# Linear attention: decays, state updates and token loads queued by edges behind the next level's preparation, and a ramp that splits weights behind tokens

## The chip, the cores and the metric

The kernel runs on one core of a Trainium2 chip. The time is device microseconds of one execution: 2990.07 us as the median of three runs (2988.25 to 2991.81). TensorE is called PE here (its weight loads PEld), VectorE DVE, ScalarE ACT, GpSimd POOL, and the engine that issues the DMAs SP.

## The reference

One layer of a diffusion transformer over 2048 latent tokens and 256 context tokens of width 1024. Gated linear attention (4 heads, key width 64, value width 128, both directions), retention, and a mixture of 16 experts follow one another. The change touches the linear attention alone, whose chunk step is this:

```python
b = jnp.cumsum(gc, axis=2)
decay = jnp.exp(jnp.where(mask, b[:, :, :, None, :] - b[:, :, None, :, :], -jnp.inf))
scores = jnp.einsum('bhik,bhjk,bhijk->bhij', qc, kc, decay)
o = jnp.einsum('bhij,bhjv->bhiv', scores, vc) + jnp.einsum('bhik,bhkv->bhiv', qc * jnp.exp(b), s)
s = jnp.exp(b_end)[:, :, 0, :, None] * s + jnp.einsum('bhjk,bhjv->bhkv', kc * jnp.exp(b_end - b), vc)
```

The tokens enter as `h = rmsnorm(x) * (1 + scale) + shift`, where scale and shift are `silu(c) @ w_ada`.

## The kernel before

Every float32 product is made of three products of rounded halves (hi times hi, hi times lo, lo times hi), so each weight and each token tile is split by a cast on ACT (`split`, L136) and a subtraction on DVE (L137).

The linear attention goes through blocks of 256 tokens, two chunks of 128 tokens in each: block 0 is the context, blocks 1 to 8 the latent tokens. `H(b)` loads a block of tokens, squares and scales them (`load`), transposes them (`pt`), modulates (`ht`), splits them (`hhi`, `hlo`) and stores them to DRAM (`hThi`, `hTlo`). `PJ(b)` makes the projections (`pk`, `pq` into `kq`; `pz` into `zt`; `pv` into `v`). `PRO(ci)` has six pieces for a chunk: G is the gate (`pg`, `ab`, `la`), C the running sums (`pcs`, `cc`), E the decayed keys (`ke`), T their transposition (`pkt`, `kd`), I the state update (`pi`, `gstate`), Q the decayed queries (`qe`, stored as `g_qe`).

`LV(ci)` computes the scores of a chunk in seven levels of half sizes 64 to 1. `prep(l)` subtracts on POOL (`dd`, L540 and L541), takes the exponential on ACT (L542), multiplies by keys and queries on DVE (`bq`, L545), and copies parts into the zero-padded `az` on ACT (L546) and POOL (L547). `level(l)` is the product `pscr` on PE and its masked copy into `st` (on ACT for level 0, L573, on DVE after, L575). `fin` is the product `po` of scores and values, copied to `ot` and stored.

The `run` lists write down the order of PE: each step's PE instructions are tied by `tc.issue_after` behind the last PE instruction before. That edge binds PE alone. A scheduler places the instructions of ACT, DVE, POOL and SP by their order in the code and by when it expects each to be ready. `tc.issue_after(ins)` gives every instruction in its block that runs on the engine of `ins` an order edge behind `ins`. An engine executes its queue in order, so an instruction that waits holds what is behind it.

The ramp is what lies before block 1. The modulation weights `ada` pass through PE (`pmod`), are copied out (`mr`, L262), transposed (`pmt`) and turned into `gsc` and `bsc`, without which no token can be modulated. The first weights of the projections are `wk` (keys), `wv` (two halves), `wq`, each loaded as two tiles `raw` of 512 KB (two buffers) and split into `whi` and `wlo`; `wz` is the small gate weight, three casts and a subtraction from `wz_raw`.

Of the kernel before, what the change touches and what calls it, by code (L numbers as in the profile page):

```python
# [8 lines left out]
F32 = mybir.dt.float32  # L9
# [5 lines left out]
OP = mybir.AluOpType  # L15
# [3 lines left out]
P = 128  # L19
# [48 lines left out]
def kernel_body(ctx, tc, a, cst, out, dbg=None, stop=None):  # L68
# [155 lines left out]
    with ExitStack() as ph:  # L224
# [36 lines left out]
        for n in range(4):  # L261
            (S.copy if n % 2 else V.tensor_copy)(mr2[:, n], pm[n][0:4])  # L262
        pmt = ptr([P, 16, 2, 2], "pmt")
# [11 lines left out]
        V.tensor_scalar(nsgn, sgn, -1.0, None, op0=OP.mult)  # L275
        wk = load_w(w_in, 3616, C_GK, W1, rp=(ad, "ada"))
        wz_raw = ad.tile([P, KC, 32], F32, name="wz_raw", tag="ada")
        wz_i = SY.dma_start(wz_raw, rows_ap(w_in, C_GZ, [[3616, P], [P * 3616, KC], [1, 32]]))

        wz_r = wz_raw.rearrange("p k (d r) -> p k d r", d=2)  # L280
        for n in range(3):
            S.copy(wz[:, :, :, n], wz_r)
        Q.tensor_tensor(wz[:, :, :, 3], wz_r, wz[:, :, :, 0].bitcast(F32), op=OP.subtract)


    with gw:
# [11 lines left out]
        w2 = g1.tile([66, 2, 256], F32R)  # L298
        w2_raw = gl.tile([66, 2, 256], F32, name="w2_raw", tag="bq", bufs=3)
        held.enter_context(tc.issue_after(wz_i.ins))  # L300
        w2_lo = gl.tile([66, 2, 256], F32R, name="w2_lo", tag="bq", bufs=3)
# [3 lines left out]
        SY.dma_start(w2_raw[64:66], rows_ap(ggb, 0, [[0, 2], [256, 2], [1, 256]]))  # L305
        split(w2, w2_lo, w2_raw, copy=V.tensor_copy, eng=Q)
        SY.dma_start(w2[16:32].bitcast(F32), w2_lo[16:32].bitcast(F32))
# [19 lines left out]
        cur = [0]  # L327
        hs, blk, chk, last = {}, {}, {}, {}

        def H(b, xs=None):  # L330
# [17 lines left out]
            def part(k2):  # L348
                def f():
# [6 lines left out]
                    for k in range(2):  # L356
# [4 lines left out]
                        else:  # L361
                            V.tensor_scalar(ht[:, k], pt[:, k], g_, b_, op0=OP.mult, op1=OP.add)
                    split(r["hi"][:, 2 * k2:2 * k2 + 2], r["lo"][:, 2 * k2:2 * k2 + 2], ht)
                return f
# [156 lines left out]
        def LV(ci):  # L521
# [5 lines left out]
            def prep(l):  # L527
                def f():
# [9 lines left out]
                    if h > 1:  # L538
                        ref = c4[:, :, h - 1:h]
                        Q.tensor_tensor(d4[:, :, h:], c4[:, :, h:], ref.to_broadcast([P, 4 * nb, h]), op=OP.subtract)  # L540
                        Q.tensor_tensor(d4[:, :, :h], ref.to_broadcast([P, 4 * nb, h]), c4[:, :, :h], op=OP.subtract)  # L541
                        S.activation(dd, dd, AF.Exp)  # L542


                        V.tensor_tensor(halves_of(bq, h), halves_of(dd, h), halves_of(kq, h), op=OP.mult)  # L545
                        S.copy(v4(az[l], F_, lo_), v4(bq, F_, lo_))  # L546
                        Q.tensor_copy(v4(az[l], B_, up_), v4(bq, B_, up_))  # L547
                    else:

                        kf, qf, kb, qb = kq[F_, 0], kq[F_, 1], kq[B_, 1], kq[B_, 0]  # L550
                        Q.tensor_tensor(d4[:, :, 0:1], c4[:, :, 1:2], c4[:, :, 0:1], op=OP.subtract)
                        S.activation(d4[:, :, 1:2], d4[:, :, 0:1], AF.Exp)
                        w4 = lambda x_, s_: x_.rearrange("p a (n x) -> p (a n) x", n=nb)[:, :, s_]
                        S.copy(v4(az[l], F_, lo_), w4(kf, lo_))
                        Q.tensor_copy(v4(az[l], B_, up_), w4(kb, up_))
                        S.mul(v4(bq, F_, lo_), w4(qf, lo_), 2.0)
                        S.mul(v4(bq, B_, up_), w4(qb, up_), 2.0)
                        V.tensor_tensor(v4(bq, F_, up_), v4(dd, F_, up_), w4(qf, up_), op=OP.mult)
                        V.tensor_tensor(v4(bq, B_, lo_), v4(dd, B_, up_), w4(qb, lo_), op=OP.mult)
                    r[l] = bq  # L560
# [25 lines left out]
            return [prep(l) for l in range(7)], [level(l) for l in range(7)], fin  # L586

        def run(*steps):

# [19 lines left out]
        h0 = H(0, xs0)  # L609
        for f in h0[:-1]:  # L610
            f()
        wv = [load_w(w_in, 3616, C_GV + 256 * i, W1) for i in range(2)]
        h0[-1]()
# [41 lines left out]
        for b in range(1, nblk):  # L655
# [6 lines left out]
            else:  # L662
                kq, z, vn, nx = [none] * 8, [none] * 2, [none] * 8, {"G": none, "C": none, "E": none}
            (_, m, f_), (pn, _, _), p, p0, p1 = lv[2 * b], lv[2 * b + 1], lv[2 * b][0], pro[2 * b], pro[2 * b + 1]
            run(fin, v[2], p[2], m[0], p1["G"], h[1], v[3], p[3], p0["T"], m[1], p0["Q"], h[2], v[4], p[4], m[2], h[3],
                p1["C"], v[5], p[5], m[3], h[4], h[5], p0["I"], p[6], m[4], v[6], pn[0], m[5], v[7], pn[1], p1["E"],
                m[6])
            fin, p, m = f_, pn, lv[2 * b + 1][1]
            pn = lv[2 * b + 2][0] if more else [none] * 2
            run(p[2], m[0], z[0], fin, z[1], kq[0], p[3], m[1], hn[0], p1["T"], p1["Q"], kq[1], kq[2], p[4], m[2],  # L670
                nx["G"], kq[3], kq[4], p[5], m[3], p1["I"])
            if b == nblk - 2:
                early_w(C_RV)
            if b == nblk - 1:
                early_w(C_RQ)
            run(kq[5], p[6], m[4], nx["C"], kq[6], kq[7], pn[0], m[5], vn[0], pn[1], nx["E"], m[6], vn[1])
            if b == nblk - 2:
# [943 lines left out]
```

## Time and profile before

| what | value |
|---|---|
| median of three runs | 2990.07 us |
| the profiled execution | 2996.73 us |
| its span in the trace | 2994.9 us |
| mean granted clock of PE | 0.979 of full speed |
| PE busy | 2842.5 us, 95% |
| DVE busy | 1953.5 us, 65% |
| ACT busy | 1304.9 us, 44% |
| POOL busy | 514.6 us, 17% |
| mean DMA rate | 185 GB/s |

The ramp takes the first 98 us or so, the linear attention of blocks 1 to 8 lasts to 540 us, retention and the output projection follow up to about 1000 us, and the rest is the router and the experts. A block takes 54 to 56 us. Shares of the whole span say little on a change that acts in a sixth of it; the stretch from 100 to 545 us has to be read by itself.

### The profile page before, as it was taken

The page shows a single profiled execution, that of the slowest core. Times are in us where ns is not written, and L with a number is a line of the kernel's source. Part 1 is how long each engine was busy: PE and PEld are TensorE (multiplying, and loading weights), DVE is VectorE, ACT ScalarE, POOL GpSimd, SP SyncE. Part 2 cuts the span into 40 slices and gives each one's busy share as a digit, 9 for nine tenths or more (in the row PEclk, how much of TensorE's full clock was granted, in tenths as well). Part 3 has the DMA queues.
Part 4 walks back from the last instruction along what each step waited for, and adds up shares of the span by engine and source line. Part 5 has one row for each costly group of instructions (what it writes and reads, how often), then busy time and mean ns, then how long its engine had stood idle before and what let it go on. Part 6 is the DMA issues. An engine that isn't in the chain of part 4 may idle for free.

```text
span 2994.9 us, 55113 instructions
## 1 busy us (share of the span) xinstructions
PE 2842.5 (95%) x21597; PEld 2687.6 (90%) x21597; DVE 1953.5 (65%) x4264; ACT 1304.9 (44%) x2310; POOL 514.6 (17%) x636
## 2 busy tenths in 40 slices
PE   6898988899999999997999999999999999999997
PEld 4888888899889999996889999999999999999996
DVE  6777777667676666656877565556565565556557
ACT  7677676332222211112334444444444444444454
POOL 1355455233121110111110000000000000000000
PEclk8999999999999999998999999999999999999999
DMA  8212114689876544434665666666566666666676
GB/s 283 79 74 113 71 64 145 204 257 275 261 226 191 180 137 131 135 102 151 202 192 181 207 209 202 201 204 219 180 219 207 203 205 197 195 203 215 200 243 247
DMA packets 458024, 554.74 MB, mean 185 GB/s; under 512 B 21126, under 2 KB 392402, under 8 KB 455460
## 3 DMA queue, kind: packets, MB, share of 16 engines
q1 hardware_dynamic: 448260, 516.61, 53.4%
q0 software_dynamic: 9504, 34.61, 4.5%
q8 instruction: 170, 2.79, 0.4%
q14 instruction: 90, 0.74, 0.1%
HBM read 458.03 MB, written 93.08 MB: 184 GB/s over the span
## 4 chain that ended last, share of the span: by engine, by line
PE 76%; DMA 6%; DVE 6%; issue 5%; ACT 4%; POOL 3%; SPq 1%; POOLq 0%; ACTq 0%; DVEq 0%
PE pau L78 31%; PE py L78 15%; PE epo L78 6%; PE epg L78 6%; PE rpq L78 4%; PE rpv L78 2%; PE pscr L78 2%; PE pv L78 1%; DMA raw<-in_w_in_dram 1%; PE xpt L83 1%; PE ept L83 1%; POOL dd L541 1%; DMA xg<-h2buf,idx 1%; POOL az L547 1%; PE rpo L78 1%
## 5 line engine op out<-in xcount | busy, mean ns | idle before, releaser
L78 PE MATMUL pau<-xlo,hig 128*128 128x256 f32 x1408 | 398.7, 283 | 0.0
L78 PE MATMUL pau<-xhi,hig 128*128 128x256 f32 x1408 | 397.8, 283 | 0.7 <-ACT xhi L136 0.4
L78 PE MATMUL pau<-xhi,lou 128*128 128x256 f32 x1408 | 396.9, 282 | 0.0
L78 PE MATMUL pau<-xlo,hiu 128*128 128x256 f32 x1408 | 396.1, 281 | 0.0
L78 PE MATMUL pau<-xhi,log 128*128 128x256 f32 x1408 | 396.0, 281 | 0.0
L78 PE MATMUL pau<-xhi,hiu 128*128 128x256 f32 x1408 | 395.1, 281 | 0.0
L1149 DVE TENSOR_TENSOR lou<-rawu,hiu 128x1024 fp32r<-128x1024 f32 x176 | 215.8, 1226 | 182.0 <-ACT hiu L1141 181.9
L1149 DVE TENSOR_TENSOR log<-rawg,hig 128x1024 fp32r<-128x1024 f32 x176 | 215.4, 1224 | 170.7 <-ACT hig L1141 170.5
L1141 ACT CAST hiu<-rawu 128x1024 fp32r<-128x1024 f32 x176 | 184.8, 1050 | 253.7 <-PE pau L78 252.0
L1149 DVE TENSOR_TENSOR lod<-rawd,hid 128x1024 fp32r<-128x1024 f32 x176 | 215.6, 1225 | 111.5 <-ACT hid L1141 111.3
L1141 ACT CAST hid<-rawd 128x1024 fp32r<-128x1024 f32 x176 | 185.1, 1051 | 226.7 <-PE py L78 226.0
L78 PE MATMUL py<-hid,hhi_e 128*128 128x512 f32 x704 | 278.7, 396 | 0.8 <-ACT hhi_e L136 0.8
L78 PE MATMUL py<-lod,hhi_e 128*128 128x512 f32 x704 | 277.5, 394 | 0.0
L1141 ACT CAST hig<-rawg 128x1024 fp32r<-128x1024 f32 x176 | 184.6, 1049 | 210.1 <-PE pau L78 208.4
L78 PEld LDWEIGHTS pau<-xhi,hig 128*128 128x128 f32 x1408 | 266.4, 190 | 8.4 <-ACT xhi L136 1.1
L78 PEld LDWEIGHTS pau<-xlo,hig 128*128 128x128 f32 x1408 | 266.7, 189 | 6.0
L78 PE MATMUL py<-hid,hlo_e 128*128 128x512 f32 x704 | 268.2, 398 | 0.0
L78 PEld LDWEIGHTS pau<-xhi,log 128*128 128x128 f32 x1408 | 267.4, 190 | 0.7
L78 PEld LDWEIGHTS pau<-xlo,hiu 128*128 128x128 f32 x1408 | 265.5, 189 | 0.8
L78 PEld LDWEIGHTS pau<-xhi,hiu 128*128 128x128 f32 x1408 | 265.1, 188 | 0.9
L78 PEld LDWEIGHTS pau<-xhi,lou 128*128 128x128 f32 x1408 | 265.1, 188 | 0.7
L1571 POOL DMA_INDIRECT xbuf<-y,idx x30 | 49.5, 1652 | 721.9 <-DVE y L1499 631.3
(437 smaller groups left out, 7683.0 us busy)
## 6 DMA issues: line engine op xcount, KB each, us to landing
rawd<-in_w_exp_down_dram SPq DMA_DIRECT2D x176, 512.0 KB
rawg<-in_w_exp_gate_dram SPq DMA_DIRECT2D x80, 1024.0 KB
rawu<-in_w_exp_up_dram SPq DMA_DIRECT2D x80, 1024.0 KB
hhi<-hThi SPq DMA_DIRECT2D x52, 512.0 KB
hlo<-hTlo SPq DMA_DIRECT2D x52, 512.0 KB
raw<-in_w_ada_dram SPq DMA_DIRECT2D x32, 512.0 KB
raw<-in_w_in_dram SPq DMA_DIRECT2D x28, 512.0 KB
hThi<-hhi SPq DMA_DIRECT2D x9, 1024.0 KB
```

The lines of the kernel that those rows point to most:

```text
L78: pe_last[0] = nc.tensor.matmul(*a_, **k_)
L83: pe_last[0] = nc.tensor.transpose(*a_, **k_)
L541: Q.tensor_tensor(d4[:, :, :h], ref.to_broadcast([P, 4 * nb, h]), c4[:, :, :h], op=OP.subtract)
L547: Q.tensor_copy(v4(az[l], B_, up_), v4(bq, B_, up_))
L1141: S.copy(hi, raw)
L1149: V.tensor_tensor(lo, raw, hi.bitcast(F32), op=OP.subtract)
L1571: Q.indirect_dma_start(out=xbuf[:, :], out_offset=bass.IndirectOffsetOnAxis(ap=idx[:, hf:hf + 1], axis=0), in_=ys[hf], in_offset=None, com ...
```

## The change

It does five things. `front` remembers the exponential and the multiplication of the latest `prep` that the code has written (`"s"` on ACT, `"v"` on DVE). `lazy(f)` puts the ACT and DVE instructions of a step behind these two; it is applied to Q, I, E of the first and second chunk of a block and to the load of the next tokens. G of the second chunk moves to the head of the block's list, and `fin` of the previous chunk two places back. In the ramp the split of `wk` is put behind the last copy `mr`, that of `wv` behind the split of the last context tokens. `wz_raw` is loaded into another buffer, later, and its casts and subtraction stand behind the first token parts, the subtraction on DVE instead of POOL; so does the subtraction of `w2`.

```diff
@@ ramp @@
-            (S.copy if n % 2 else V.tensor_copy)(mr2[:, n], pm[n][0:4])
+            mi = (S.copy if n % 2 else V.tensor_copy)(mr2[:, n], pm[n][0:4])
...
-        wk = load_w(w_in, 3616, C_GK, W1, rp=(ad, "ada"))
-        wz_raw = ad.tile([P, KC, 32], F32, name="wz_raw", tag="ada")
-        wz_i = SY.dma_start(wz_raw, rows_ap(w_in, C_GZ, [[3616, P], [P * 3616, KC], [1, 32]]))
-
-        wz_r = wz_raw.rearrange("p k (d r) -> p k d r", d=2)
-        for n in range(3):
-            S.copy(wz[:, :, :, n], wz_r)
-        Q.tensor_tensor(wz[:, :, :, 3], wz_r, wz[:, :, :, 0].bitcast(F32), op=OP.subtract)
+        with tc.issue_after(mi.ins):
+            wk = load_w(w_in, 3616, C_GK, W1, rp=(ad, "ada"))
...
+        wz_raw = gl.tile([P, KC, 32], F32, name="wz_raw", tag="ot", bufs=1)
+        wz_i = SY.dma_start(wz_raw, rows_ap(w_in, C_GZ, [[3616, P], [P * 3616, KC], [1, 32]]))
...
-        split(w2, w2_lo, w2_raw, copy=V.tensor_copy, eng=Q)
+        split(w2, w2_lo, w2_raw, copy=V.tensor_copy)
...
-                    split(r["hi"][:, 2 * k2:2 * k2 + 2], r["lo"][:, 2 * k2:2 * k2 + 2], ht)
+                    front["hi"], front["lo"] = split(r["hi"][:, 2 * k2:2 * k2 + 2], r["lo"][:, 2 * k2:2 * k2 + 2], ht)
@@ prep @@
-                        S.activation(dd, dd, AF.Exp)
+                        front["s"] = S.activation(dd, dd, AF.Exp)
-                        V.tensor_tensor(halves_of(bq, h), halves_of(dd, h), halves_of(kq, h), op=OP.mult)
+                        front["v"] = V.tensor_tensor(halves_of(bq, h), halves_of(dd, h), halves_of(kq, h), op=OP.mult)
...
+        def lazy(f):
+            def g():
+                with tc.issue_after(front["s"].ins), tc.issue_after(front["v"].ins):
+                    f()
+            return g
@@ ramp @@
-        for f in h0[:-1]:
+        for f in h0[:3]:
             f()
-        wv = [load_w(w_in, 3616, C_GV + 256 * i, W1) for i in range(2)]
+        wz_r = wz_raw.rearrange("p k (d r) -> p k d r", d=2)
+        for n in range(3):
+            S.copy(wz[:, :, :, n], wz_r)
+        V.tensor_tensor(wz[:, :, :, 3], wz_r, wz[:, :, :, 0].bitcast(F32), op=OP.subtract)
+        for f in h0[3:-1]:
+            f()
+        with tc.issue_after(front["hi"].ins), tc.issue_after(front["lo"].ins):
+            wv = [load_w(w_in, 3616, C_GV + 256 * i, W1) for i in range(2)]
@@ blocks @@
-            run(fin, v[2], p[2], m[0], p1["G"], h[1], v[3], p[3], p0["T"], m[1], p0["Q"], h[2], v[4], p[4], m[2], h[3],
-                p1["C"], v[5], p[5], m[3], h[4], h[5], p0["I"], p[6], m[4], v[6], pn[0], m[5], v[7], pn[1], p1["E"],
+            run(p1["G"], v[2], fin, p[2], m[0], h[1], v[3], p[3], p0["T"], m[1], lazy(p0["Q"]), h[2], v[4], p[4], m[2], h[3],
+                p1["C"], v[5], p[5], m[3], h[4], h[5], lazy(p0["I"]), p[6], m[4], v[6], pn[0], m[5], v[7], pn[1], lazy(p1["E"]),
                 m[6])
...
-            run(p[2], m[0], z[0], fin, z[1], kq[0], p[3], m[1], hn[0], p1["T"], p1["Q"], kq[1], kq[2], p[4], m[2],
-                nx["G"], kq[3], kq[4], p[5], m[3], p1["I"])
+            run(p[2], m[0], z[0], fin, z[1], kq[0], p[3], m[1], lazy(hn[0]), p1["T"], lazy(p1["Q"]), kq[1], kq[2], p[4], m[2],
+                nx["G"], kq[3], kq[4], p[5], m[3], lazy(p1["I"]))
...
-            run(kq[5], p[6], m[4], nx["C"], kq[6], kq[7], pn[0], m[5], vn[0], pn[1], nx["E"], m[6], vn[1])
+            run(kq[5], p[6], m[4], nx["C"], kq[6], kq[7], pn[0], m[5], vn[0], pn[1], lazy(nx["E"]), m[6], vn[1])
```

The instructions stand in another order on their engines. Lines of the new kernel up to `prep` are four lower than before (L538 is the exponential L542, L541 the multiplication L545, L470 the keys L474).

First place: ACT in block 3, from the sums `cc` of the second chunk to its first exponentials `dd`. Before:

```order
L457 COPY cc<-pcs 64x2x128 x2
L556 ACTIVATE bq<-kq 64x256
L557 ACTIVATE bq<-kq 64x256
L505 ACTIVATE qe<-cc,pcols 128x512
L360 ACTIVATE ht<-pt,bsc,gsc 128x256 x2
L342 ACTIVATE sq,ss<-xt_2816 128x1024
L467 ACTIVATE eall<-et 128x4
L474 ACTIVATE ke<-cc,et,nsgn 128x128 x4
L494 COPY gstate_505<-pi 64x512
L542 ACTIVATE dd<-dd 128x512
L136 CAST hhi<-ht 128x512
L542 ACTIVATE dd<-dd 128x512
```

Now (`sq` is the load step of the next tokens, `eall` the chunk's end decay):

```order
L453 COPY cc<-pcs 64x2x128 x2
L136 CAST hhi<-ht 128x512
L463 ACTIVATE eall<-et 128x4
L552 ACTIVATE bq<-kq 64x256
L553 ACTIVATE bq<-kq 64x256
L356 ACTIVATE ht<-pt,bsc,gsc 128x256 x2
L538 ACTIVATE dd<-dd 128x512
L490 COPY gstate_501<-pi 64x512
L136 CAST hhi<-ht 128x512
L538 ACTIVATE dd<-dd 128x512
L470 ACTIVATE ke<-cc,et,nsgn 128x128 x4
L538 ACTIVATE dd<-dd 128x512
```

The queries `qe`, the keys `ke` and the squares `sq` stood ahead of the first `dd`; now a `dd` comes first, `ke` follows the second, and `sq` and `qe` come after the fourth.

Second place: DVE at the end of block 3, around the last masked copies `st` of its second chunk. Before:

```order
L575 COPY_PREDICATED st<-lmask,pscr 128x512
L476 TENSOR_TENSOR ke<-ke,kq 64x512
L477 TENSOR_TENSOR ke<-ke,kq 64x512
L394 TENSOR_SCALAR kq<-pq_3002 64x2x128
L575 COPY_PREDICATED st<-lmask,pscr 128x512
L394 TENSOR_SCALAR kq<-pq_3002 64x2x128
L507 TENSOR_TENSOR qe<-qe,kq 64x512
L545 TENSOR_TENSOR bq<-dd,kq 128x2x4x64
L545 TENSOR_TENSOR bq<-dd,kq 128x2x8x32
```

Now:

```order
L390 TENSOR_SCALAR kq<-pq_3002 64x2x128
L571 COPY_PREDICATED st<-lmask,pscr 128x512
L390 TENSOR_SCALAR kq<-pq_3002 64x2x128
L541 TENSOR_TENSOR bq<-dd,kq 128x2x4x64
L541 TENSOR_TENSOR bq<-dd,kq 128x2x8x32
L571 COPY_PREDICATED st<-lmask,pscr 128x512
L472 TENSOR_TENSOR ke<-ke,kq 64x512
L473 TENSOR_TENSOR ke<-ke,kq 64x512
```

The two `ke` stood ahead of the last `st`, and the first `bq` of block 4 behind it; now two `bq` and the `st` come first, `ke` behind.

Third place: the ramp, first ACT from the last `ada` cast on. Before:

```order
L136 CAST adahi<-ada 128x1024 x4
L136 CAST whi<-raw 128x1024
L262 COPY mr_400<-pmod_233 4x512
L136 CAST whi<-raw 128x1024 x3
L262 COPY mr_400<-pmod_235 4x512
L282 CAST wz<-wz_raw 128x16x16 x3
L360 ACTIVATE ht<-pt,bsc,gsc 128x256 x2
L136 CAST hhi<-ht 128x512 x2
```

Now:

```order
L136 CAST adahi<-ada 128x1024 x4
L262 COPY mr_400<-pmod_233 4x512
L262 COPY mr_400<-pmod_235 4x512
L136 CAST whi<-raw 128x1024 x2
L356 ACTIVATE ht<-pt,bsc,gsc 128x256 x2
L136 CAST hhi<-ht 128x512 x2
L356 ACTIVATE ht<-pt,bsc,gsc 128x256 x2
L618 CAST wz<-wz_raw 128x16x16 x3
L136 CAST hhi<-ht 128x512 x2
L136 CAST whi<-raw 128x1024 x2
```

Two of the four `whi` (those of `wv`) moved behind the four token splits `hhi`, both `mr` ahead of the other two, and the `wz` casts between the second and the third token part.

The DMA queue of the same stretch, from the constants on. Before:

```order
L314 DMA lmf<-const_lmask_dram 128x512
L314 DMA lmf<-const_lmask_dram 128x256
L166 DMA raw<-in_w_in_dram 128x4x256 x2
L307 DMA w_470<-w_lo 16x512
L308 DMA w_470<-w_lo 1x16x32
L367 DMA hThi_78<-hhi 128x2048
L166 DMA raw<-in_w_in_dram 128x4x256
L368 DMA hTlo_87<-hlo 128x2048
```

Now:

```order
L310 DMA lmf<-const_lmask_dram 128x512
L310 DMA lmf<-const_lmask_dram 128x256
L363 DMA hThi_78<-hhi 128x2048
L303 DMA w_464<-w_lo 16x512
L304 DMA w_464<-w_lo 1x16x32
L364 DMA hTlo_87<-hlo 128x2048
L166 DMA raw<-in_w_in_dram 128x4x256 x4
```

The second half of `wv`, which went out ahead of the token stores, now goes out behind them, since its two buffers come free only when the first half has been split.

## Rows read from the trace of the kernel before

**Rows 1.** The page, chain that ended last, shares of the span.

```profile
PE 76%; DMA 6%; DVE 6%; issue 5%; ACT 4%; POOL 3%; SPq 1%; POOLq 0%; ACTq 0%; DVEq 0%
```

**Rows 2.** Busy time by stretch: A:B, length, engines, PEclk, DMA share, GB/s.

```profile
200.00:250.00 50.00, 44.29 (x364) 43.49 (x363) 38.93 (x70) 37.17 (x85) 28.50 (x38) 0.97 0.25 96
239.00:244.00 5.00, 4.79 (x28) 4.79 (x29) 3.63 (x9) 2.74 (x8) 4.63 (x8) 0.66 0.52 211
268.00:272.00 4.00, 3.04 (x24) 2.86 (x25) 3.90 (x7) 1.71 (x4) 1.86 (x2) 1.00 0.18 66
600.00:650.00 50.00, 49.04 (x407) 48.21 (x406) 32.56 (x81) 16.75 (x47) 16.78 (x17) 1.00 0.93 273
```

**Rows 3.** What PE waited for, 100 to 545 us: total, times, longest.

```profile
PE pscr L78 <- POOL az L547: 34.0, 15, 3.7
PE pcs L78 <- DVE la L445: 7.6, 7, 1.8
PE po L78 <- DVE st L575: 6.3, 8, 1.4
PE pq L78 <- DVE kq L394: 3.0, 2, 1.6
```

**Rows 4.** Timeline of PE in block 3: start, length, instruction, [wait before <-releaser].

```profile
213.21 1.13 PE L78 MATMUL po<-v,st 128*128 128x128 f32 x8 [0.43 <-DVE st L575]
...
216.36 1.16 PE L78 MATMUL pscr<-bq,az 128*128 128x128 f32 x8 [0.60 <-POOL az L547]
...
225.13 1.16 PE L78 MATMUL pcs<-tri,la 128*128 128x128 f32 x8 [0.96 <-DVE la L445]
...
239.21 1.83 PE L78 MATMUL pscr<-bq,az 128*128 128x128 f32 x8 [3.72 <-POOL az L547]
...
268.37 1.13 PE L78 MATMUL po<-v,st 128*128 128x128 f32 x8 [1.39 <-DVE st L575]
...
274.62 0.60 PE L83 MATMUL pkt<-ident,ke 128*128 128x128 f32 x4
```

**Rows 5.** Timeline of ACT, 227 to 238 us.

```profile
227.75 0.74 ACT L457 COPY cc<-pcs 64x256 f32<-64x256 f32 x2
...
229.58 0.72 ACT L505 ACTIVATE qe<-cc,pcols 128x512 f32<-128x512 f32 x1
...
231.24 1.05 ACT L342 ACTIVATE sq<-xt 128x1024 bf16<-128x1024 f32 x1
...
232.38 1.64 ACT L474 ACTIVATE ke<-cc,et,nsgn 128x128 f32<-128x128 f32 x4
...
234.65 0.63 ACT L542 ACTIVATE dd<-dd 128x512 f32<-128x512 f32 x1
```

**Rows 6.** Timeline of POOL, 229 to 239 us.

```profile
229.21 0.61 POOL L541 TENSOR_TENSOR dd<-cc 128x256 f32<-128x256 f32 x1
...
237.91 1.25 POOL L547 COPY az<-bq 64x256 f32<-64x256 f32 x1 [1.51 <-ACT dd L542]
```

**Rows 7.** Timeline of DVE, 264 to 269 us.

```profile
264.90 1.21 DVE L476 TENSOR_TENSOR ke<-ke,kq 64x512 f32<-64x512 f32 x1 [0.88 <-ACT ke L474]
...
267.50 0.72 DVE L575 COPY_PREDICATED st<-lmask,pscr 128x512 f32<-128x512 uint8 x1
```

**Rows 8.** Groups by line and shape, 100 to 545 us: busy us, mean ns.

```profile
L541 POOL TENSOR_TENSOR dd<-cc 128x256 f32<-128x256 f32 x94 | 78.0, 829 | 0.0
```

**Rows 9.** Timelines of the ramp: ACT, DVE, then two rows of PE.

```profile
36.01 2.94 ACT L136 CAST whi<-raw 128x1024 fp32r<-128x1024 f32 x3
...
42.66 4.62 DVE L137 TENSOR_TENSOR wlo<-raw,whi 128x1024 fp32r<-128x1024 f32 x4
...
48.84 0.58 PE L78 MATMUL pk<-hlo,whi 128*128 128x256 f32 x1 [3.76 <-DVE hlo L137]
...
63.45 0.37 PE L78 MATMUL pv<-whi,hhi 128*128 128x256 f32 x1
```

**Rows 10.** The chain of waits in the ramp: start, length, piece.

```profile
47.13 5.30 DMA raw<-in_w_in_dram
```

More of the change, by code (lines that the diff above doesn't have):

```diff
@@ L327, in kernel_body @@
         cur = [0]
-        hs, blk, chk, last = {}, {}, {}, {}
+        hs, blk, chk, last, front = {}, {}, {}, {}, {}
         def H(b, xs=None):
@@ L551, in f @@
                         Q.tensor_tensor(d4[:, :, 0:1], c4[:, :, 1:2], c4[:, :, 0:1], op=OP.subtract)
-                        S.activation(d4[:, :, 1:2], d4[:, :, 0:1], AF.Exp)
+                        front["s"] = S.activation(d4[:, :, 1:2], d4[:, :, 0:1], AF.Exp)
                         w4 = lambda x_, s_: x_.rearrange("p a (n x) -> p (a n) x", n=nb)[:, :, s_]
@@ L558, in f @@
                         V.tensor_tensor(v4(bq, F_, up_), v4(dd, F_, up_), w4(qf, up_), op=OP.mult)
-                        V.tensor_tensor(v4(bq, B_, lo_), v4(dd, B_, up_), w4(qb, lo_), op=OP.mult)
+                        front["v"] = V.tensor_tensor(v4(bq, B_, lo_), v4(dd, B_, up_), w4(qb, lo_), op=OP.mult)
                     r[l] = bq
```

## The prediction

> **What bounds the kernel now.** I read the page's chain first: three quarters of the end hang on PE itself [rows 1], so a change on other engines pays only where PE waits. The busy times by stretch come next. Between 200 and 250 us PE is busy 44.29 of 50 us and no other engine exceeds 39, while in 600:650 it is busy 49.04 of 50 [rows 2]. In the linear attention PE therefore waits for chains that cross several engines, and not for one engine that is full; behind it, in the retention, PE is the bound itself and whatever is gained before should be passed on. The list of PE's waits from 100 to 545 us names them. Those for `az`, `la`, `st` and `kq` make 34.0 + 7.6 + 6.3 + 3.0 = 50.9 us [rows 3]. That is the stock the change can draw on, with the clock and the ramp.
>
> The timeline of PE shows where the waits lie in a block. Block 3 has 0.43 us before its first `po`, 0.60 before the first `pscr`, 0.96 before the `pcs` of its second chunk, and 3.72 before the first `pscr` of that chunk; block 4 opens with 1.39 before its `po` [rows 4]. So a block loses 5.71 us with its own first `po` and 6.67 with that of the next. I go by six blocks of this pattern (2 to 7; the ends differ): 6 x 6.19 = 37.1 of the 50.9 us.
>
> Why 3.72 is visible on ACT and POOL. The sums `cc` are copied at 227.75 us, POOL ends its second `dd` of the top level at 229.21 + 0.61 = 229.82, but ACT reaches the exponential only at 234.65 [rows 5, 6]. In between stand, among others, `qe` (0.72), `sq` (1.05) and `ke` (1.64), which nobody needs yet [rows 5]. The `az` copy then runs at 237.91 for 1.25 us, and PE starts at 239.21 [rows 4, 6].
>
> **The change, part by part.** All sums are made against the profiled execution of 2996.73 us, which lies 6.66 above the median of 2990.07; the forecast is moved by that at the end.
>
> First the edges on ACT in the middle of a block. The order puts `qe`, `sq` and `ke` behind the exponentials, 0.72 + 1.05 + 1.64 = 3.41 us off the path from `cc` to `az`. The wait of 3.72 becomes 0.31 if nothing else takes their place. The new order puts one `hhi` cast of the tokens ahead of `cc`'s followers, and ACT is busy 37 of 50 us [rows 2], so I take 0.75, with 0 and 3 as the bounds (3: the cc copy itself comes no earlier, and ACT's backlog of rows 5 fills the hole).
>
> Second, DVE at the end of a block. Two `ke` multiplications, the first 1.21 us long from 264.90, hold the `st` that starts at 267.50, and PE waits 1.39 for it [rows 4, 7]. They now stand behind it, yet two `bq` are ahead of it and wait for ACT's exponentials. I take 0.6 left, between 0 and 2. What is late next is `ke` itself: its readers are the transposition `pkt`, at 274.62 on PE [rows 4]. The `st` that follows both `ke` starts at 267.50, so they have some 7 us to spare; two `bq` of about the length of a `ke`, and a `st` of 0.72, use 3 to 4 of it. I cost this at nothing.
>
> Third, the gate. `pg` goes ahead of 24 `pv` and the `po`, so `la` is ready earlier, and the wait of 0.96 before `pcs` goes; DVE has `ke` out of its way in the same place. The 0.60 before the first `pscr` and the 0.43 go with the second point. So six blocks keep 0.75 + 0.6 each: 37.1 - 6 x 1.35 = 29.0 us gained, between 6 x (6.19 - 5) = 7 and 37.
>
> Fourth, what is left of the 50.9 us, 13.8, lies in block 1, block 8 and scattered spots that the same edges touch but that I didn't follow. Bounds 0 and 13.8; I take a third, 5, since the edges act on `az` and `st` alike but the `kq` wait has no edge of its own.
>
> Fifth, the clock. From 239 to 244 us, right behind the wait of 3.72, the granted clock is 0.66; behind the wait of 1.39, from 268 to 272, it is 1.00 [rows 2]. PE does at 0.66 what takes 3.3 us at full clock, so 1.7 us a block, in agreement with the mean of 0.97 over 200:250 (0.03 x 50 = 1.5). Six blocks make 10. With the wait at 0.75 the drop should stay away, but waits may join up with others: I take half, 5, of 0 to 10.
>
> Sixth, the ramp. Before `hhi` of the tokens ACT casts weights for 2.94 us (three `whi`), and DVE subtracts four `wlo` in 4.62 us [rows 9]. Half of these, and the first `whi` ahead of an `mr`, leave the token path; PE's wait of 3.76 at 48.84 for the first `hlo` [rows 9] should go, and `pk` start 4 to 6 us earlier. Against this, the second half of `wv` loses its place in the DMA queue. Its load of 5.30 us ran from 47.13 to 52.43 [rows 10], and PE first uses that half at 63.45 [rows 9]. Now it is issued only after the first half is split, which itself waits behind the last `hhi` and `hlo`, and behind 2 MB of token stores. I estimate its landing near 61, its split near 63, while PE, being earlier, would want it at 58 to 59. So the 4 to 6 us won are given back there, and I take 0, between 4 lost and 4 gained. The casts of `wz` in ACT's queue ahead of the third `hhi` belong to the same uncertainty.
>
> The sum: 29 + 5 + 5 + 0 = 39, so 2996.73 - 39 = 2957.7 for a profiled execution, and 2957.7 - 6.7 = 2951 against the median.
>
> [...] POOL's `dd` took 0.61 us at 229.21 [rows 6] but 0.829 on average over 94 [rows 8]; `bq` and `ke`, DVE operations with two inputs, run in that time. [...] This is weighed as the first rival.
>
> **The rivals.** (A) As summed: 2951; its own range, with each bound taken in part, 2937 to 2968. Chance 0.60.
>
> (B) The waits come back in another place. If a `dd` pair on POOL goes from 0.61 to twice its length per instruction because DVE's `bq` and `ke` now run beside it, and ACT's deferred `qe`, `sq`, `ke` fall due together in the following levels, then about 3 us a block return: 6 x 3 = 18, and the clock's 5 with them. Gain 39 - 23 = 16: 2996.7 - 16 - 6.7 = 2974, with 2968 to 2984 around it. For it: ACT is at 37 and DVE at 39 of 50 us, so little room is left in a block [rows 2]. Against it: the mean `dd` of 0.829 already contains such meetings. A second way to the same number is the retention's loads, with the DMA at 0.93 in 600:650 [rows 2]: if they don't start earlier, PE gets there sooner and waits. Chance 0.16.
>
> (C) Everything goes: 50.9 + 10 of clock + 4 of ramp = 65, or 2925 against the median; waits that PE had in the cover of longer ones make this rare. Its neighbourhood down from 2937 has 0.09.
>
> (D) No change: the scheduler placed the old order by its own readiness times, and the removed wait is replaced by one of the same size, such as the copy of `cc` that ACT reaches as late as before. 2990, chance 0.08. Against it stands the direct sum of 3.41 us of unneeded work on the path [rows 5].
>
> (E) Slower by the deferred keys. `ke` now waits on ACT behind the exponentials and on DVE behind the `bq` that need them; `pkt` follows on PE's fixed order, and PE has nothing else to do while it waits. The margin is 7 us, of which 3 to 4 are used. Once `ke` slips by more than 7 us, every further one is lost in each of 16 chunks; from about 2.5 us beyond the margin the 39 are eaten, and at 3.2 beyond it is 16 x 3.2 - 39 = 12 slower, 3002. For it: the edge binds to the latest `prep` written in the code, whatever its time. Against it: `ke` stands behind two exponentials, not more. Chance 0.07.
>
> **How the numbers follow.** About 0.2%, 6 us, is what a measurement of this kernel can tell from no change. A, B and C are faster by more than that: 0.85; D is the same, 0.08; E slower, 0.07. The forecast is A's 2951. The range leaves out E, D and the far end of C: from 2930, in the middle of C, to 2983, the end of B.
>
> **What would show it.** PE's waits for `az` between 100 and 510 us should fall from 34.0 us below 12, those for `la` and `st` below 3 each. On ACT the first exponential of a block's second chunk should stand within about 3 us of `cc`. The granted clock of these blocks should rise from 0.97 to 0.98 or more. In the ramp the first `pk` with `hlo` should come at 42 to 45 us, and a new wait of `pv` for `wlo` or `whi` of the second half near 60 us. From the last `po` to the end the length should be unchanged. I am wrong if the wait at the second chunk's first `pscr` stays above 2.5 us, if `pkt` or `pi` shows up among PE's waits, or if the retention gives back what came before it.

## The result and the profile after

| | before | after |
|---|---|---|
| median of four runs, us | 2990.94 (2988.25 to 2991.81) | 2955.45 (2953.02 to 2963.87) |
| the profiled execution, us | 2996.73 | 2955.36 |
| first to last `po` (linear attention), us | 406.8 | 365.6 |
| last `po` to last `rpo` (retention), us | 444.5 | 441.4 |
| last `rpo` to first `pau` (projection, router), us | 446.7 | 444.8 |
| first `pau` to last `py` (experts), us | 1546.9 | 1553.7 |

The ratio is 0.9888 with a 95% interval of 0.9867 to 0.9909: 35.5 us faster by the medians, 41.4 by the two profiled executions. The stretches are taken from the start times of these products in each trace. All of the gain lies in the linear attention; the experts, whose code was not touched, lost 6.8 us, and the two stretches between gained 5.0.

Busy times by stretch of the kernel after, same columns as [rows 2]:

```profile
200.00:250.00 50.00, 47.65 (x407) 47.06 (x407) 42.98 (x77) 40.72 (x94) 30.46 (x43) 1.00 0.24 96
239.00:244.00 5.00, 5.00 (x45) 5.00 (x45) 3.75 (x10) 2.18 (x6) 0.00 (x0) 1.00 0.07 25
```

PE does 407 products in the 50 us in which it did 364, at the full clock, and is busy 47.65 of 50 us instead of 44.29 [rows 2]. What PE waited for from 98 to 545 us, answering to [rows 3] (lines are four lower now):

```profile
PE pq L78 <- DVE kq L390: 7.7, 6, 1.6
PE po L78 <- DVE st L571: 5.8, 7, 1.0
PE pscr L78 <- POOL az L543: 3.6, 3, 1.9
PE pscr L78 <- DVE st L571: 3.6, 9, 1.4
...
PE po L78 <- DVE lg L656: 1.3, 1, 1.3
...
PE pscr L78 <- ACT az L550: 0.7, 1, 0.7
PE pcs L78 <- DVE la L441: 0.6, 1, 0.6
PE pt L83 <- DVE tt L652: 0.5, 1, 0.5
```

The wait for `az` fell from 34.0 to 3.6 us, that for `la` from 7.6 to 0.6; that for `kq` rose from 3.0 to 7.7. These eight make 23.8 us, those for `lg` and `tt` in block 1 (the last `po` starts at 496 us; the rows left out belong to what comes behind it). Of [rows 3] the four named there made 50.9, and two smaller ones of 1.4 and 0.8 us, for `st`, belong to the same list: 53.1. So 29 us of waits are gone. Block 3 on PE, answering to [rows 4]:

```profile
205.48 1.06 PE L78 MATMUL po<-v,st 128*128 128x128 f32 x8
...
213.73 1.06 PE L78 MATMUL pcs<-tri,la 128*128 128x128 f32 x8
...
224.26 1.13 PE L78 MATMUL pscr<-bq,az 128*128 128x128 f32 x8 [0.26 <-DVE st L571]
...
227.33 1.16 PE L78 MATMUL po<-v,st 128*128 128x128 f32 x8 [1.00 <-DVE st L571]
...
238.75 0.36 PE L78 MATMUL pq<-hhi,whi 128*128 128x256 f32 x1 [1.09 <-DVE kq L390]
```

The `pcs` has no wait, the first `pscr` of the second chunk (224.26) waits 0.26 us instead of 3.72, and no longer for `az`. A block has two `po`, and the wait has moved from one to the other. The one at its head (205.48) waits for nothing now; at the head of block 4 it waited 1.39 us before [rows 4]. The one of the block's first chunk (`fin` in the second list, 227.33) waits 1.00 us for `st`; before, it came behind the wait of 3.72 and had none of its own:

```profile
242.55 1.23 PE L78 MATMUL po<-v,st 128*128 128x128 f32 x8
```

All of the 5.8 us for `st` in the list above are waits of this second kind.

On ACT, answering to [rows 5]:

```profile
216.06 0.74 ACT L453 COPY cc<-pcs 64x256 f32<-64x256 f32 x2
216.83 0.62 ACT L136 CAST hhi<-ht 128x512 fp32r<-128x512 f32 x1
...
218.36 1.02 ACT L356 ACTIVATE ht<-pt,bsc,gsc 128x256 f32<-128x256 f32 x2
219.28 0.63 ACT L538 ACTIVATE dd<-dd 128x512 f32<-128x512 f32 x1
...
221.59 1.63 ACT L470 ACTIVATE ke<-cc,et,nsgn 128x128 f32<-128x128 f32 x4
```

From `cc` to the first exponential it is 3.22 us (216.06 to 219.28), where it was 6.90 (227.75 to 234.65 in [rows 5]): the keys come 2.3 us behind it. In the ramp three rows of PE answer to [rows 9]:

```profile
44.71 0.58 PE L78 MATMUL pk<-hlo,whi 128*128 128x256 f32 x1 [1.69 <-DVE hlo L137]
...
62.03 0.39 PE L78 MATMUL pv<-wlo,hhi 128*128 128x256 f32 x1 [1.34 <-DVE wlo L137]
...
73.21 0.80 PE L78 MATMUL pg<-w,zt 66*128 66x256 f32 x2 [4.66 <-ACT cc L453]
```

The first `pk` with `hlo` starts 4.1 us earlier (48.84 before). The split of `wv` then costs 1.34 us at 62.03, and at 73.21 `pg` waits 4.66 us for a copy of `cc`: the first `po` starts at 130.5, against 132.4 before. That gain of 1.9 us is not the ramp's: with the ramp of before and the rest of the change (e4) the first `po` starts at 129.9, with the new ramp alone (e1) at 135.4.

### The profile page after: what moved, and what is told of

Read it like the earlier page. It is cut to its first block, busy times and chain, and to the rows that moved or that the text cites. A ratio compares the mean times of both kernels' runs of the same rounds, so it can differ in the third digit from the quotient of the medians.

```text
span 2953.6 us, 55123 instructions
## 1 busy us (share of the span) xinstructions
PE 2829.6 (96%) x21596; PEld 2675.2 (91%) x21597; DVE 1951.0 (66%) x4266; ACT 1300.9 (44%) x2310; POOL 515.0 (17%) x634
## 4 chain that ended last, share of the span: by engine, by line
PE 74%; DMA 7%; DVE 7%; issue 7%; ACT 3%; SPq 1%; POOL 1%; POOLq 0%; DVEq 0%; ACTq 0%
PE pau L78 29%; PE py L78 14%; PE epo L78 6%; PE epg L78 6%; PE rpq L78 4%; PE rpv L78 2%; PE pscr L78 2%; PE pq L78 2%; DMA xg<-h2buf,idx 1%; PE pv L78 1%; PE xpt L83 1%; PE ept L83 1%; PE pk L78 1%; DVE st L571 1%; DMA raw<-in_w_ada_dram 1%
## 5 line engine op out<-in xcount | busy, mean ns | idle before, releaser
L78 PE MATMUL pau<-xhi,lou 128*128 128x256 f32 x1408 | 396.6, 282 | 0.0
```

Source lines behind the costliest of these rows:

```text
L78: pe_last[0] = nc.tensor.matmul(*a_, **k_)
```

## The experiments

Every kernel was timed in five rounds beside the kernel before (2988.48 to 2991.38 us in these sets; each ratio is against its own set). The stretches of each one's trace, which decide more than the totals:

| kernel | median us | first to last `po` | to last `rpo` | to first `pau` | experts |
|---|---|---|---|---|---|
| before | 2990.94 | 406.8 | 444.5 | 446.7 | 1546.9 |
| after | 2955.45 | 365.6 | 441.4 | 444.8 | 1553.7 |
| e1 ramp only | 2992.07 | 407.9 | 441.4 | 444.8 | 1544.9 |
| e2 lists only | 2972.92 | 389.3 | 437.4 | 444.4 | 1545.6 |
| e3 edges only | 2960.64 | 371.3 | 440.1 | 445.6 | 1554.6 |
| e4 lists and edges | 2953.05 | 363.8 | 442.7 | 444.3 | 1552.3 |
| e5 edge on keys only | 2967.93 | 377.8 | 439.6 | 445.4 | 1552.6 |
| e6 no edge on keys | 2943.67 | 364.0 | 439.5 | 444.7 | 1544.6 |
| e7 fin later | 2937.34 | 359.7 | 438.3 | 445.1 | 1545.7 |
| e8 fin and load later | 2960.96 | 371.1 | 439.7 | 445.3 | 1553.6 |
| e9 gather first | 2952.78 | 366.2 | 438.7 | 445.5 | 1552.1 |
| e10 fin later, no key edge | 2949.02 | 365.7 | 437.5 | 445.8 | 1544.3 |
| e11 filled wait | 2973.69 | 396.6 | 437.7 | 444.5 | 1542.1 |
| e12 tokens behind copy | 2935.31 | 355.9 | 439.7 | 446.3 | 1544.0 |

**The parts of the change.** The first four each keep one part (e1, e2, e3) or two (e4).

```diff
 e1: the lists of before, no lazy(...); the ramp of the change
 e2: the ramp of before, no lazy(...)
-            run(fin, v[2], p[2], m[0], p1["G"], h[1], v[3], ...
+            run(p1["G"], v[2], fin, p[2], m[0], h[1], v[3], ...
 e3: the ramp and the lists of before, with
-  p0["Q"], p0["I"], p1["E"], hn[0], p1["Q"], p1["I"], nx["E"]
+  each of them as lazy(...)
 e4: e2 and e3 together
```

> Only the ramp of the change, with the lists of before and no edges in the blocks. Theory 1 (the edges free the first exponentials and the last masked copies; the ramp gives and takes the same): 2987 to 2995 us against 2991, the waits for az between 98 and 545 us stay at 30 us or more, pcs for la at 7 or more, the granted clock of 200:250 stays at 0.97. Theory 2 (a good part of the gain, and of the clock, comes from the ramp): 2981 or less, and the stretch of 100:150 us, which was at 0.90, alone rises to 0.98 or more.

Measured 2992.07 us, ratio 1.0005 (0.9996 to 1.0014), `az` 35.7 us, `la` 6.4, a little less than the 7 expected; the clock of 200:250 was 0.93, not better than the 0.97 of before. The ramp is worth nothing by itself, as theory 1 had it.

> Only the lists of the blocks (the gate of the second chunk first, fin two places later), with the ramp of before and no edges. Theory 1: the lists take away the wait of pcs for la (7.6 us), nothing of az (34.0, stays above 28); 2980 to 2987 us. Rival (the place of the gate decides, since cc, and with it the whole second chunk, comes earlier; the edges are decoration): az falls below 15, 2965 or less. Granted clock of 200:250: 0.97 by theory 1, 0.99 or 1.00 by the rival.

Measured 2972.92, ratio 0.9946 (0.9932 to 0.9959): 18 us, more than theory 1 gave, less than the rival. PE's waits from 98 to 545 us in this kernel:

```profile
PE pscr L78 <- issue: 18.5, 5, 3.7
PE pscr L78 <- POOL az L547: 18.3, 10, 3.1
...
PE pcs L78 <- DVE la L445: 0.6, 1, 0.6
```

The two `pscr` rows together, 36.8 us, are the old wait for `az` (34.0), now partly without a releaser that the profile names. In its block 2 the sums `cc` are copied at 171.40 us and the first exponential starts at 177.46, 6.06 us later, with `qe`, `sq` and `ke` still in between. So the gate's place does not free the exponentials. It takes away the 7.6 us for `la`, and the wait of `po` for `st`, which I had given to the edges, is down to 0.2 from 6.3.

> Only the edges in the blocks, with the ramp and the lists of before. Theory 1: az falls from 34.0 to below 10 us, la keeps 5 or more of its 7.6, the clock of 200:250 rises to 0.99 or more; 2962 to 2970 us. Rival (without the earlier gate the cc copy comes as late as before and ACT's backlog fills the hole): az above 20, 2978 or more.

Measured 2960.64, ratio 0.9897 (0.9882 to 0.9913), 1.4 us below theory 1's interval. The waits:

```profile
PE pcs L78 <- DVE la L445: 13.3, 9, 4.0
...
PE pscr L78 <- POOL az L547: 2.5, 2, 2.2
```

The edges alone remove `az`, and nearly double `la`: with the exponentials served first, the gate is late. That is why the lists have to move with the edges.

> Lists and edges of the change, with the ramp of before. Theory 1: as the whole change, 2952 to 2960 us; az below 6, la below 2 in total. Rival (the ramp carries a part): 2965 or more. If the parts add up, this gain is that of the lists alone and that of the edges alone together, within 4 us.

Measured 2953.05, ratio 0.9876 (0.9859 to 0.9894), as theory 1 had it. The parts do not add up: against the 2989.34 of before in that set, 16.4 and 28.7 apart make 45.1, together 36.3. In the linear attention alone it is 17.5 + 35.5 = 53.0 against 43.0.

**Which edges.** Both keep the lists and the ramp of the change.

```diff
 e5
-  lazy(p0["Q"]), lazy(p0["I"]), lazy(hn[0]), lazy(p1["Q"]), lazy(p1["I"])
+  p0["Q"], p0["I"], hn[0], p1["Q"], p1["I"]
 e6
-  lazy(p1["E"]), lazy(nx["E"])
+  p1["E"], nx["E"]
```

> The whole change, but only the decayed keys (E) of both chunks keep their edge; Q, I and the next load are placed by the scheduler. Between the lists alone (2972.9 us) and the whole change (2955.5) lie 17.4 us. Theory 1 (each microsecond of unneeded work ahead of the first exponential on ACT counts alike): the keys are 1.64 of the 3.41 us, 48%, so about 2964 us, az about 15 to 20 us in total. Rival (the keys decide, since they also hold the masked copies on DVE): 2958 or less, az below 8.

> The whole change with the edges on Q, I and the next load, but none on the keys (E). Theory 1: 52% of the 17.4 us, about 2964 us. Rival (the keys decide): 2969 or more, with waits for st on DVE as well as for az. If E alone and the others alone each give nearly all, the edges overlap: both 2958 or less.

Measured 2967.93 us, ratio 0.9928 (0.9915 to 0.9942), and 2943.67, ratio 0.9853 (0.9838 to 0.9868). Neither is the 2964 of theory 1, and the wait for `az` in e5 is 22.9 us, above its 15 to 20. By the totals the edge on the keys would cost 12 us (2955.45 against 2943.67). The stretches say otherwise: from first to last `po` it is 365.6 with it and 364.0 without, so 1.6 of the 12; the rest lies behind the last `po`, 9.1 us of it in the experts. From the 389.3 us of the lists alone, the keys' edge by itself takes 11.5, the others by themselves 25.3, all together 23.7. (The 389.3 are with the ramp of before; e1 puts the difference at about 1 us.) The share of 48% for the keys comes out where they stand alone (11.5 of 23.7), but the shares do not add up: the others alone take all of it, and with them in place the keys add nothing. So theory 1, by which each microsecond ahead of the exponential counts alike, does not hold here.

**Why the experts differ.** In the table their stretch is either 1542 to 1547 or 1552 to 1555 us. The scheduler places all instructions of the program by when it expects them to be ready, so another order in the linear attention gives another one far behind. The kernel after, DVE, POOL and PE at the place where the second expert's tokens are gathered:

```profile
1483.27 0.16 DVE L1436 COPY ax<-pl 128x10 f32<-128x10 f32 x1
1483.35 2.71 DVE L1510 SCALAR_TENSOR_TENSOR y<-py,gate,m 128x512 f32<-128x512 f32 x4
...
1487.19 0.15 DVE L1438 SCALAR_TENSOR_TENSOR idx<-ax 128x2 int32<-128x2 f32 x1
...
1485.04 1.66 POOL L1582 DMA_INDIRECT xbuf<-y,idx  x1 [11.55 <-DVE y L1510]
...
1488.25 1.02 POOL L1445 DMA_INDIRECT xg<-h2buf,idx  x1 [0.15 <-issue]
...
1493.82 0.66 PE L83 MATMUL xpt<-ident,xg 128*128 128x128 f32 x2 [10.97 <-DMA xg<-h2buf,idx]
```

The same place in e7 (fin later), where the order is that of before:

```profile
1470.92 0.17 DVE L1436 COPY ax<-pl 128x10 f32<-128x10 f32 x1
...
1471.12 0.16 DVE L1438 SCALAR_TENSOR_TENSOR idx<-ax 128x2 int32<-128x2 f32 x1
...
1476.47 0.44 PE L83 MATMUL xpt<-ident,xg 128*128 128x128 f32 x2 [1.41 <-DMA xg<-h2buf,idx]
...
1479.81 1.54 PE L83 MATMUL xpt<-ident,xg 128*128 128x128 f32 x6 [2.90 <-DMA xg<-h2buf,idx]
```

Between `ax` and the list `idx` lie 3.92 us in the one (four `y` of the expert before, and a weight's subtraction) and 0.20 in the other; PE waits 10.97 us and once more 0.60, against 4.31 in the two waits of e7. The other kernels fall into the same two groups. In the eight with the shorter experts `idx` follows `ax` after 0.20 us and these waits of PE make 3.7 to 4.3 us; in the six with the longer ones they make 10.1 to 12.5, and in all but e9 `y` stands between `ax` and `idx`. e9 adds two edges to the kernel after (`oi` computes `idx` of the next expert, `gi` is its last gather; the loop over `hf` holds the weighing and the scatter):

```diff
-            for hf in range(2):
+            with ExitStack() as behind:
+                if e == 0:
+                    behind.enter_context(tc.issue_after(nxt["oi"].ins))
+                    behind.enter_context(tc.issue_after(nxt["gi"].ins))
+                for hf in range(2):
...
```

> The whole change, and in the experts the weighing of expert 0's output (y on DVE) and its scatter (xbuf on POOL) are put by an edge behind expert 1's list (idx) and gather (xg). Theory: the experts, which the change doesn't touch, lost 7 us because the scheduler placed y and xbuf ahead of idx and xg there: PE's wait of 10.97 us for xg at 1494 falls to 5 to 7, and the time from 2955.5 to 2949 to 2951; from the first pau to the last py 1547 to 1550 us instead of 1553.7. Rival (that wait is a matter of when the lists are routed, not of this order): within 2 us of 2955.5, the wait above 9.

Measured 2952.78, ratio 0.9882 (0.9869 to 0.9895); PE's wait went from 10.97 to 8.58:

```profile
1484.66 0.16 DVE L1436 COPY ax<-pl 128x10 f32<-128x10 f32 x1
1486.05 0.15 DVE L1438 SCALAR_TENSOR_TENSOR idx<-ax 128x2 int32<-128x2 f32 x1
1486.19 2.72 DVE L1511 SCALAR_TENSOR_TENSOR y<-py,gate,m 128x512 f32<-128x512 f32 x4
```

The edge did what it should, `idx` follows `ax` after 1.39 us now, but it brought 2.4 us of that wait and not the 4 to 6 expected, and the second wait grew from 0.60 to 1.56 us, so that 1.4 us are left, and 1.6 over the experts as a whole. The time lies between the theory's 2949 to 2951 and the rival's 2953.5 and more: the order of `y` and `idx` is the smaller part. What goes with the rest is that `ax` itself is late: the product `pl` that it copies starts 99.9 to 101.0 us after the first `pau` in the six kernels with the longer experts (100.0 in the kernel after, 101.0 in e9), but 95.2 to 96.9 in the other eight (96.0 before, 96.2 in e7). What in the order delays `pl` was not tried, so that part of the cause stays open.

**The clock.** e11 is the kernel before with 24 products that serve nothing, put into the wait of 3.72 us, in each of blocks 1 to 7.

```diff
-            run(p[2], m[0], z[0], fin, ...
+            run(p[2], fill, m[0], z[0], fin, ...     # fill: 24 products into pz
```

> The kernel before, with 24 products more on PE (into pz, which the true projection then overwrites) ahead of the first pscr of each second chunk, blocks 1 to 7: some 2.8 us of work in the wait of 3.72 for az. Theory (the drop to 0.66 of the granted clock behind that wait comes of PE standing idle in it): the wait shrinks to about 0.9 without PE getting on sooner, the clock of 239:244 stays at 1.00, and 168 products more make the kernel 8 to 12 us faster, 2978 to 2982. Rival (the clock has another cause, such as the other engines' work): 2989 or more, 0.66 still there.

Measured 2973.69, ratio 0.9953 (0.9941 to 0.9965): 168 products more, and 15 us less. First PE's busy time by stretch, then the row behind the fill:

```profile
200.00:250.00 50.00, 46.54 (x394) 45.72 (x393) 40.07 (x71) 37.66 (x86) 28.98 (x39) 1.00 0.25 96
237.00:242.00 5.00, 4.84 (x41) 4.84 (x42) 3.76 (x8) 2.84 (x9) 4.71 (x7) 1.00 0.53 218
```

```profile
237.16 1.16 PE L78 MATMUL pscr<-bq,az 128*128 128x128 f32 x8 [0.89 <-POOL az L556]
```

The other engines do the same as before in the five microseconds behind the wait, and the clock is 1.00 there instead of 0.66 [rows 2]. The time is 4 us below the interval of the theory. The linear attention gains 10.2 us by this alone (406.8 to 396.6). It is not the waits that give them: those from 98 to 545 us fall from 53.1 to 33.0, but the fill takes those 20 us itself, 168 products 0.12 us apart. By the granted clock of the stretches from 100 us on, what it lacked times their length goes from 14.5 to 5.0 us, an estimate of 9.5. Behind the linear attention the profiled execution is shorter as well (4.8 us in the experts, 9.0 in the two stretches between), where nothing was filled. So the price of the long waits was their length and this.

**Going on.** e7 and e8 attack what was left; e10 and e12 build on e7.

```diff
 e7
-            run(p[2], m[0], z[0], fin, z[1], kq[0], p[3], m[1], lazy(hn[0]), ...
+            run(p[2], m[0], z[0], z[1], fin, kq[0], p[3], m[1], lazy(hn[0]), ...
 e8: e7, and lazy(hn[0]) behind m[3]
 e10: e7, and no lazy on E
 e12: e7, and lazy(hn[0]) behind kq[1], with
+                with tc.issue_after(front["k"].ins):    # the last kq copy; from the third block on
                     V.tensor_scalar(r["x"][i], r["x"][i], rs[:, i:i + 1], ...)
```

> The whole change, and po of the first chunk's scores (fin in the second list) goes behind the second half of the pz projection, whose 8 products run 0.12 us apart, so 1 to 2 us later. What is left of po's wait for st, 5.8 us in 7 (1.0 the longest), should fall below 1; 2950 us against 2955.5, if nothing else moves. Rival (PE just reaches its next wait sooner, that of pq for kq): the pq wait grows from 7.7 by as much, and the time stays within 2 us.

Measured 2937.34, ratio 0.9827 (0.9815 to 0.9840). The linear attention takes 359.7 instead of 365.6 us, 5.9 less, where 5.8 of waits were to go; 8.0 more lie in the experts, in their shorter order. That is why the total is 13 us below the 2950 expected.

> As the kernel before in this list, and the load step of the next tokens goes from behind m[1] to behind m[3] of the second chunk, so that the scaling of xt (1.42 us on DVE) no longer stands ahead of the kq copies that pq waits for. The wait of pq for kq (7.7 us in 6) should fall below 2: another 6 us, 2944 us. Rival (the tokens come late then: pt waits for xt at the head of the next block, 0.5 us or more in each of 7 blocks): 2950 or more, with a new wait of pt.

Measured 2960.96, ratio 0.9902 (0.9889 to 0.9915), in the rival's range and with its new wait of `pt`. PE's waits, 98 to 500 us:

```profile
PE pq L78 <- DVE kq L390: 11.0, 7, 1.7
PE pt L83 <- ACT ht L356: 4.0, 6, 0.7
PE pscr L78 <- ACT az L542: 3.8, 6, 0.6
```

The tokens come late to `pt`, and the wait for `kq` grew too, which neither side expected. In block 3 `xt` does stand behind the first copies on DVE now, but DVE waits 2.95 us for ACT's part of them (`kq` on ACT at 238.59), and there the two squares `sq` of the load step (235.41 to 237.49) run ahead of it. The long order of the experts adds 7.9 us against e7.

> fin behind the whole pz projection, and no edge on the keys. Theory (in the linear attention the edge on the keys is worth nothing: 364.0 us from the first to the last po without it and 365.6 with it; the 12 us by which it seemed to cost were the experts' other order): first to last po 357 to 360 us, as the 359.7 with fin later alone, and 2935 to 2940 us in all. Rival (the edge on the keys costs by itself, and the two gains add): 2927 or less.

Measured 2949.02, ratio 0.9873 (0.9858 to 0.9889), 365.7 us from first to last `po`. Both were wrong: with `fin` later the edge on the keys is worth 6.0 us (359.7 with it), though without that change it is worth nothing. In e10 PE waits 9.2 us for `az` (0.77 us in each of blocks 2 to 7 before the second chunk's first `pscr`) where e7 has 2.6 and one of 1.5 without a releaser, but 5.9 instead of 8.2 for `kq`; all its waits make 20.0 us against 17.6. So 2.4 of the 6.0 us are waits, and I have no cause for the rest.

> The whole change with fin later (2937.3 us), and the scaling of the next tokens (xt, two instructions, 1.42 us on DVE) is put by an edge behind the last kq copy of the first pk, on which pq waits; the load step stands behind kq[1] in the list. Theory (that wait, 8.2 us in 7, is the 1.42 us of xt in DVE's queue): it falls below 2, first to last po from 359.7 to 352 to 355 us, 2929 to 2933 in all. Rival (the wait moves to the next in the queue: la for pcs, or the second pk's copies for pq): 2935 or more.

Measured 2935.31, ratio 0.9815 (0.9798 to 0.9832), 355.9 us from first to last `po`:

```profile
PE pt L83 <- ACT ht L357: 4.1, 5, 0.8
...
PE pq L78 <- DVE kq L391: 1.8, 2, 1.6
```

The wait of `pq` for `kq` fell from 8.2 to 1.8, so it was the 1.42 us of `xt` in front of the copy; but 4.1 us came back as a new wait of `pt` for `ht`, not at the places that the rival named. 3.8 us of the linear attention are gained, a little less than expected (355.9 against 352 to 355), and the total is in the rival's range of 2935 or more. In the total it cannot be told from e7, since the two intervals overlap. Both beat the kernel after.

## Why the prediction was right, point by point

The forecast was 2951 us within 2930 to 2983; measured were 2955.45. The sum of 39 us stands against 41.4 in the profiled executions. The mechanism was right. That the sum came out so near is in part luck: the waits were put 5 us too high and the clock 8 too low, and the two errors cancel. Its terms:

The edges on ACT: 0.75 us was to be left of 3.72; it is 0.26, and e2 and e3 show that it is the edges and not the gate. By the reasoning on `cc` alone the 3.41 us of unneeded work came off whole: 6.90 - 3.22 = 3.68 between `cc` and the first exponential.

DVE at the end of a block: 0.6 was to be left of the 1.39 before the `po` at the head of the next block. Nothing is left (205.48); the lists alone have `po` at 0.2 us in all and the edges alone at 1.4 for `st`. What came instead is the wait of the other `po`, 0.8 to 1.0 us in each of blocks 2 to 7 and 0.25 in block 8, 5.8 in all. The `st` for which it waits ran on DVE at 226.55 in block 3, right behind the two `ke` of the second chunk (224.61 to 226.52). The sum has no such term; only rival B said in general that waits come back in another place.

The gate: 0.96 gone, as said.

Waits in all: 29 + 5 = 34 forecast, 29 measured. The `kq` wait without an edge of its own was named; that it would grow from 3.0 to 7.7 was not.

The clock is the term that was mis-sized most. I took 5 of 0 to 10. The granted clock of the nine stretches between 100 and 540 us, 0.90 to 1.00, lost 14.5 us before, by an estimate (the sum of what each lacked, times its length); after, up to 500 us where the linear attention ends, it is 1.5. That makes 13, more than the upper bound. Filling the wait alone gave 10.2. With the 29 us of waits it is 42, against 41.2 between the first and the last `po` and 1.9 ahead of it. The half that I held back for waits that join up did not exist: no wait longer than 1.9 us is left in these blocks.

The ramp: 0 forecast, no difference in the total measured (e1, though its first `po` starts 3.0 us later than before, within the bound of 4 lost), and by the path that was described: `hlo` 4.1 us earlier, given back to `wlo` and then, not foreseen, to `pg`.

What follows the linear attention was to be unchanged. Its length is 2457.5 us against 2455.7, but by two opposite moves that the forecast did not have: the experts' 6.8 us, which is the scheduler's other order there, and 5.0 less in the two stretches before. These two together vary from 881.8 to 891.2 us over the 14 kernels without a pattern that I can tie to the change; the 891.2 are those of the kernel before, whose profiled execution lies above its median.

Last, the step from the profile to the median. I took 6.7 us off because the profile of before lay that much above its median. The profile of after lies on its median. The 41.4 us between the profiles are therefore 35.5 between the medians, and the forecast came out 4.5 us low though the sum was 2.4 us short.

Of the signs named beforehand one failed: the waits for `st` were to fall below 3 us, and 9.4 are left (5.8 before `po`, 3.6 before `pscr`). The others came: `az` at 3.6 and `la` at 0.6 us, an exponential 3.22 us behind `cc`, the clock at 1.00, `hlo` at 44.71, a wait of `pv` at 62.03, and neither `pkt` nor `pi` among PE's waits.

Of the rivals, B had POOL's `dd` lengthen. The second of the pair took 0.829 us on average before [rows 8] and 0.816 after, the first 0.788 and 0.852, and the `bq` beside them 0.768 and 0.837. Two rows of before, then three of after:

```profile
L540 POOL TENSOR_TENSOR dd<-cc 128x256 f32<-128x256 f32 x94 | 74.0, 788 | 83.5 <-ACT cc L457 62.2 <-DVE hlo L137 14.9 <-DVE bq L559 2.5
L545 DVE TENSOR_TENSOR bq<-dd,kq 128x512 f32<-128x512 f32 x96 | 72.5, 768 | 18.9 <-ACT dd L542 18.9
```

```profile
L536 POOL TENSOR_TENSOR dd<-cc 128x256 f32<-128x256 f32 x95 | 81.0, 852 | 79.4 <-ACT cc L453 75.6
L541 DVE TENSOR_TENSOR bq<-dd,kq 128x512 f32<-128x512 f32 x96 | 79.1, 837 | 5.6 <-ACT az L542 4.6
...
L537 POOL TENSOR_TENSOR dd<-cc 128x256 f32<-128x256 f32 x96 | 78.4, 816 | 0.0
```

So both engines' instructions became longer in sum: DVE 69 ns x 96 = 6.6 us, POOL 64 - 13 = 51 ns a pair, some 5 us. The doubling from 0.61 us, out of which B had its 3 us a block, neither trace shows: the means after are the 0.852 and 0.816. How much of the lengthening reaches PE no run shows. Two `bq` and a `dd` of the kernel after show it singly:

```profile
183.06 0.62 POOL L547 TENSOR_TENSOR dd<-cc 128x256 f32<-128x256 f32 x1
...
183.12 1.10 DVE L541 TENSOR_TENSOR bq<-dd,kq 128x512 f32<-128x512 f32 x1
...
188.48 0.67 DVE L541 TENSOR_TENSOR bq<-dd,kq 128x512 f32<-128x512 f32 x1
```

Alone (188.48) it takes 0.67, started 0.06 us behind a `dd` 1.10. The 0.43 us more are most of the 0.56 that the `dd` still had to run. Two more in this trace go the same way: with 0.53 us of a `dd` to run a `bq` took 1.07 us, 0.40 more (171.57), with 0.31 to run 0.86, 0.19 more (207.52). Why they lengthen when they meet was not shown. As a reason against the change it did not carry, since little is waited for `az` any more (3.6 and 0.7 us). E, the late keys, did not come: `pkt` is not among PE's waits. D is excluded by the interval.

## What to carry to other kernels

Where an engine in the middle of a chain executes in order, find what stands ahead of the instruction that the bottleneck waits for; here 3.4 us of work that nobody needed yet stood there in each block, and putting it behind took away, with the earlier gate, 29 us of waits and 13 us of slow clock (an estimate). Read an edit's effect from its own stretch: with a scheduler that places the whole program, an edit in one stage reorders another, and here that shift (7 to 9 us) was as large as what was to be told apart. Edges on one engine and the order of another belong together: each alone left the wait that the other took away.

## What the runs showed of the hardware

The granted clock of PE went with its own waiting in these two kernels: before, behind a wait of 3.72 us, it was 0.66 over 5 us [rows 2]; in e11, with about the same work on DVE, ACT and POOL (3.76, 2.84 and 4.71 us busy of 5, against 3.63, 2.74 and 4.63) and throwaway products on PE up to 0.89 us before the end of the wait, it was 1.00. The 168 products more made the kernel 15 us faster by the medians, and the linear attention 10.2 us shorter in the profiled executions.

PE kept to the order of its queue: in the kernel before, it stood idle for the 3.72 us up to the `pscr` at 239.21 [rows 4], and `pz`, whose tokens were split by 238.45 (the end of this `hlo`), came behind it:

```profile
237.77 0.68 DVE L137 TENSOR_TENSOR hlo<-ht,hhi 128x512 fp32r<-128x512 f32 x1
...
240.70 0.56 PE L78 MATMUL pz<-hhi,wz 128*128 128x256 f32 x1
```

In e11 the 24 products into the same tile, placed ahead of that `pscr`, ran in the wait, from 233.16 to 236.28.
